# Down weights stored in the steps' order, early additions without priority, and a rearranged last normalization, in a two-layer decoder trunk

## The chip, the core and the metric

The kernel runs on one core of a Trainium2 chip. The metric is the device time of one execution, in microseconds. The engines are PE (TensorE, matmuls; PEld is its weight load), DVE (VectorE), ACT (ScalarE), POOL (GpSimd) and SP (SyncE, which here issues nearly all DMAs). Each engine works through its own instructions in order and waits on semaphores for the others. PSUM, into which TensorE writes, has eight banks.

## The reference

The reference is a decoder trunk of two layers on a sequence of 1024 positions with 1024 channels. Each layer adds a mixer and then a dense MLP to the residual h, each behind an RMS norm, and a last RMS norm gives the output:

```python
for layer in range(DEPTH):
    y = _rms_norm(h, mix_norm_g[layer])
    ...                      # gated spatial mixer, then dilated attention
    h = h + y
    y = _rms_norm(h, mlp_norm_g[layer])
    h = h + jnp.square(jax.nn.relu(y @ w_up[layer])) @ w_down[layer]
return _rms_norm(h, final_norm_g)
```

The hidden width is 4096. Everything is float32 and h is held transposed: eight tiles h[0] to h[7] of 128 channels by 1024 positions.

## The kernel before

**Products.** A float32 matmul is made from three matmuls of a reduced type: each operand is split into a high part (a ScalarE copy, line 205) and a low part (source minus high part, on VectorE, line 206), and high·high, high·low and low·high are added in PSUM (`three`). Weights appear in the profile as `wp` when split and as `r` when just loaded; hidden activations as `hx` when split and `t` when loaded.

**The MLP.** Both products of the MLP are done with seven block products in place of eight, each a 2x2 scheme (Strassen-like, with the terms numbered 1 to 7 in the code). For every group of weights, `Weights` loads four blocks into staging buffers (SP, line 169), GpSimd forms four sums and differences (lines 410, 411, 412 and 415), and ScalarE and VectorE split seven blocks in the order 4, 1, 2, 5, 6, 7, 3. The `steps` of the next group are called between the products of the present one, so one group is prepared while the other is multiplied.

**The down projection** (`Down.run`) goes through 18 steps t. Step t works for output rows a = t mod 4, that is the tiles h[a] and h[a + 4], and sums over a window of up to four hidden groups: one group in step 0, two in step 1, three in step 2, four from step 3 on. The groups are taken in the order 14, 0, 1, 2 ... 13, since 14 is still on the chip when the up projection ends; the others are read back from DRAM (`hid`). Within a step the products go in the order of terms 5, 6, 1, 7, 3, 2, 4. Term 5 writes a PSUM bank d, which is then added to one half of h[a + 4] (`add(1, 1, d)`, line 940); term 3 accumulates into the same bank, and d is added to another half (`add(0, 1, d)`). Terms 7 and 4 share a bank e, terms 1 and 2 a bank a. So term 3 waits for the addition that follows term 5, and term 4 for the one that follows term 7. Term 6 goes with an accumulator u that lives across steps (lines 954, 962, 963, 966).

**What sets the order.** TensorE's order is written out by the program as it runs through a simple model of time. The orders of the other engines come from a list scheduler with its own estimates, in which `tc.high_priority` moves an instruction forward. The additions to h on VectorE had this priority in every step; the splits of weights and hidden tiles had none. SP's order comes from the same scheduler.

**The end.** After step 17 the hidden group 15 is multiplied (`close`), first for positions 0 to 511, then for 512 to 767, then for 768 to 1023. After each piece `final` normalizes it: squares of h, sums over channels by matmuls with a vector of ones, `rsqrt` (a root on ScalarE and five small VectorE instructions, lines 236 to 246), a `spread` of the result over a PSUM bank by transposes on TensorE (line 187), and the products, each followed by a store. Some tiles, those in `far`, are multiplied by GpSimd (line 1591): ScalarE has multiplied them by the gain (line 1579), and GpSimd multiplies by `pc`, a copy of the spread that ScalarE makes in SBUF (line 1586). The others go through VectorE (line 1593), which reads the spread in PSUM. In the last piece (`Direct`) the sums run along with the matmuls: each block of 128 positions has a PSUM bank of its own, and VectorE copies the two columns together (line 309).

Of the kernel before, what the change touches and what calls it, by code (L numbers as in the profile page):

```python
# [12 lines left out]
AF = mybir.ActivationFunctionType  # L13
# [4 lines left out]
P = 128  # L18
D = 1024
S = 1024  # L20
HALF = 512
KT = D // P
# [11 lines left out]
def blk(b, n=1):  # L34
    return slice(b * P, (b + n) * P)
# [69 lines left out]
PRIO = 60  # L105
# [7 lines left out]
def trunk(ctx: ExitStack, tc: tile.TileContext, xT, w_u, w_v, w_o, w_s, b_s, w_qkv, w_bo, rel,  # L113
          w_up, w_dn, w_dl, vecs, onehot, outT):
    nc = tc.nc
# [12 lines left out]
    def temp():  # L128
        return tpool.tile([P, HALF], F32, tag="t", name="t", bufs=NT)
# [46 lines left out]
    def at_bank():  # L176
        return psa.tile([P, HALF], F32, tag="at", name="at")

    def matmul(out, lhsT, rhs, passes=1, **kw):
        nc.tensor.matmul(out, lhsT, rhs, **kw)  # L180
        n = 1
        for d in rhs.shape[1:]:
            n *= d
        flow.pe(max(n, 64) * COL * passes)
# [9 lines left out]
    ones = const.tile([P, P], F32, name="ones")  # L194
# [34 lines left out]
    def rsqrt(src, scale, out=None, power=False):  # L229

        n = src.shape[1]
        v = small.tile([P, n], F32, tag="rv", name="rv")
        r = small.tile([P, n], F32, tag="rr", name="rr")
        if not power:
            sd = small.tile([P, n], F32, tag="sd", name="sd")
            nc.scalar.activation(sd, src, AF.Sqrt, bias=eps, scale=scale)
        nc.vector.tensor_scalar(v, src, scale, EPS, op0=ALU.mult, op1=ALU.add)
        if power:
            nc.gpsimd.tensor_tensor(r, v, mhalf[:, 0:n], op=ALU.pow)
        else:  # L240
            nc.vector.reciprocal(r, sd)
        a = small.tile([P, n], F32, tag="ra", name="ra")
        nc.vector.tensor_tensor(a, r, v, op=ALU.mult)
        nc.vector.scalar_tensor_tensor(a, a, -0.5, r, op0=ALU.mult, op1=ALU.mult)
        q = small.tile([P, n], F32, tag="rq", name="rq") if out is None else out
        nc.vector.scalar_tensor_tensor(q, a, 1.5, r, op0=ALU.add, op1=ALU.mult)
        return q
# [37 lines left out]
    class Direct(Square):  # L285


        def __init__(self, cols):
            super().__init__(cols)
            self.parts, self.ps = [], [at_bank() for _ in range(self.n // P)]  # L290

        def add(self, k):
            sq = temp()[:, 0:self.n]
# [3 lines left out]
                self.sum(k - 2)  # L297

        def sum(self, k):
            for b, ps in enumerate(self.ps):  # L300
                matmul(ps[:, 0:1], self.parts[k][:, blk(b)], ones[:, 0:1], passes=2, start=k == 0, stop=k == KT - 1)

        def rms(self, out=None):
            for k in range(KT - 2, KT):
                self.sum(k)
            with tc.high_priority(offset=PRIO):
                v = temp()[:, 0:len(self.ps)]
                for b, ps in enumerate(self.ps):
                    nc.vector.tensor_copy(v[:, b:b + 1], ps[:, 0:1])
                return rsqrt(v, 1.0 / D, out)  # L310

    def spread(r):

# [570 lines left out]
    class Down:  # L884
# [12 lines left out]
        def weights(self, t, **kw):  # L897
            a, ks = self.todo[t]

            runs = []  # L900
            for k in (self.order[i] for i in ks):
                if runs and k == runs[-1][1]:
                    runs[-1][1] += 1
                else:
                    runs.append([k, k + 1])
            return Weights(lambda i, j: [w_dn[self.layer, a, i, j][:, lo * P:hi * P] for lo, hi in runs], **kw)

        def take(self, k, src, which):
            for p in which:
# [16 lines left out]
        def run(self, w):  # L926
            for t, (a, ks) in enumerate(self.todo):
# [8 lines left out]
                    return [self.x[self.order[k]][p] for k in ks]  # L936

                def add(i, s, src, engine=nc.vector):
                    with tc.high_priority(offset=PRIO if engine is nc.vector else 0):
                        engine.tensor_tensor(hs[i, s], hs[i, s], src, op=ALU.add)  # L940

                if t == 16:
# [630 lines left out]
    def final(sq):  # L1573
        n, far = HALF // sq.n, {}

        for k in {0: (1, 3, 5), 512: (0, 4), 768: (0,)}[sq.cols.start]:
            far[k] = temp().rearrange("p (k t) -> p k t", k=n)
            for i in range(n):
                nc.scalar.activation(far[k][:, i, :], h[k + i][:, sq.cols], AF.Copy, scale=vec[:, 4, k + i:k + i + 1])
        r = sq.rms()  # L1580
        yield LAT["rms"]
        pb = spread(r)
        out = outT.rearrange("(k p) t -> p k t", p=P)
        pc = spare()[:, 0:sq.n] if far else None
        if far:
            nc.scalar.activation(pc, pb[:, 0:sq.n], AF.Copy)
        for k in range(0, KT, n):
            t = far[k] if k in far else temp().rearrange("p (k t) -> p k t", k=n)
            for i in range(n):
                if k in far:  # L1590
                    nc.gpsimd.tensor_tensor(t[:, i, :], t[:, i, :], pc, op=ALU.mult)
                else:
                    nc.vector.scalar_tensor_tensor(t[:, i, :], h[k + i][:, sq.cols], vec[:, 4, k + i:k + i + 1],
                                                   pb[:, 0:sq.n], op0=ALU.mult, op1=ALU.mult)
            nc.sync.dma_start(out[:, k:k + n, sq.cols], t)
            yield LAT["out"]
# [73 lines left out]
```

## Time and profile before

| | us |
|---|---|
| median of 3 runs | 2140.34 |
| lowest, highest | 2135.99, 2142.17 |
| profiled execution | 2137.66 |
| its span, first to last instruction | 2135.9 |
| TensorE busy in the span | 2103.7 (98%) |
| VectorE, ScalarE, GpSimd busy | 1602.5, 1117.9, 561.8 |

Layer 0's down projection begins at about 611 us and layer 1's at about 1808 us; the last piece's sums end near 2125.6 us. In a row of a profile `h<-h,at` reads: the instruction writes a tile named h from a tile h and a PSUM tile at; `128x512` is partitions by elements; `x3` a count; a bracket gives the idle time of the engine before the instruction, and what ended it. The names at and mm are PSUM banks.

### The profile page before, as it was taken

How to read it: one execution, taken by the hardware profiler on the slowest of the kernel's cores; microseconds unless marked ns; L12 is line 12 of the kernel's file. 1: busy time of each engine (PE TensorE's matmuls, PEld its weight loads, DVE VectorE, ACT ScalarE, POOL GpSimd, SP SyncE). 2: the span in 40 equal slices, each digit the busy share in tenths (PEclk: the TensorE clock that was granted, in tenths of full speed). 3: DMA queues.
4: the chain of work that ended last, by engine and by line, in shares of the span. 5: the costliest groups of instructions: out<-in, count | busy, mean ns of one | idle time of the engine just before them, and what ended most of it. 6: DMA issues, size and time to landing. Idle time of an engine off the chain costs nothing.

```text
span 2135.9 us, 30439 instructions
## 1 busy us (share of the span) xinstructions
PE 2103.7 (98%) x10426; PEld 1742.5 (82%) x10426; DVE 1602.5 (75%) x2918; ACT 1117.9 (52%) x2262; POOL 561.8 (26%) x417
## 2 busy tenths in 40 slices
PE   8999999999999999999999999999999999999998
PEld 7888887888878888887888788888888887888887
DVE  7975258577689888888676867768876667988886
ACT  6644136554574444356666656665555546544443
POOL 2100213233323322531212122201133332332345
PEclk9999999999999999999999999999999999999999
DMA  6411114455354443311112021141155543544432
GB/s 220 141 64 50 40 42 136 161 183 188 129 183 163 158 159 129 103 79 52 46 46 55 32 57 41 47 146 68 52 175 182 194 153 133 192 162 138 142 107 79
DMA packets 158815, 247.07 MB, mean 116 GB/s; under 512 B 33481, under 2 KB 47940, under 8 KB 158660
## 3 DMA queue, kind: packets, MB, share of 16 engines
q1 hardware_dynamic: 158336, 244.94, 35.2%
q8 instruction: 82, 1.34, 0.3%
q14 instruction: 73, 0.60, 0.1%
q10 hardware_dynamic: 324, 0.18, 0.0%
HBM read 180.41 MB, written 64.66 MB: 115 GB/s over the span
## 4 chain that ended last, share of the span: by engine, by line
PE 89%; DVE 6%; ACT 3%; issue 1%; DMA 1%; SPq 0%; DVEq 0%; ACTq 0%
PE at L180 43%; PE mm L180 43%; PE at L187 2%; DVE wp L206 1%; DMA t<-hid 1%; DVE t L206 1%; ACT t L1272 1%; DVE h L340 0%; ACT wp L205 0%; DVE y L206 0%; DVE h L940 0%; DVE tr L206 0%; DVE raws L498 0%; SPq L169 0%; DVE hx L206 0%
## 5 line engine op out<-in xcount | busy, mean ns | idle before, releaser
L205 ACT ACTIVATE wp<-r 128x512 fp32r<-128x512 f32 (+3 forms) x490 | 294.4, 605 | 460.4 <-PE at L180 286.3
L180 PE MATMUL at<-hx,wp 128*128 128x512 f32 x1770 | 413.7, 389 | 3.9 <-DVE wp L206 2.3
L206 DVE TENSOR_TENSOR wp<-r,wp 128x512 fp32r<-128x512 f32 (+3 forms) x490 | 372.7, 764 | 39.3 <-ACT wp L205 36.1
L180 PE MATMUL mm<-y,wp 128*128 128x512 f32 x1608 | 398.2, 393 | 2.3 <-ACT t L1132 1.1
L180 PEld LDWEIGHTS at<-hx,wp 128*128 128x128 f32 x1770 | 331.8, 188 | 75.1 <-DVE h L940 3.3
L180 PEld LDWEIGHTS mm<-y,wp 128*128 128x128 f32 x1608 | 299.3, 188 | 67.8 <-DVE h L340 1.6
L180 PE MATMUL at<-t,wp 128*128 128x512 f32 x1344 | 314.0, 389 | 0.7 <-DVE t L803 0.7
L180 PEld LDWEIGHTS at<-t,wp 128*128 128x128 f32 x1344 | 252.3, 188 | 53.4 <-DVE t L803 1.1
L410 POOL TENSOR_TENSOR t<-r 128x512 f32<-128x512 f32 (+3 forms) x78 | 113.6, 1456 | 679.9 <-DMA r<-in_w_dn 258.5
L412 POOL TENSOR_TENSOR r<-r 128x512 f32<-128x512 f32 (+3 forms) x77 | 113.0, 1468 | 377.6 <-DVE wp L206 344.8
L180 PE MATMUL mm<-t,wp 128*128 128x512 f32 x768 | 191.5, 396 | 0.0
L206 DVE TENSOR_TENSOR hx<-t,hx 128x512 fp32r<-128x512 f32 x192 | 181.0, 955 | 5.5 <-ACT hx L205 5.4
L180 PE MATMUL mm<-hx,wp 128*128 128x512 f32 x708 | 171.7, 389 | 0.0
L180 PEld LDWEIGHTS mm<-t,wp 128*128 128x128 f32 x768 | 140.5, 188 | 29.7 <-DVE t L1207 0.2
L269 POOL TENSOR_TENSOR t<-t 128x512 f32<-128x512 f32 (+1 forms) x54 | 72.3, 1339 | 346.3 <-ACT t L258 344.4
L180 PE MATMUL mm<-y,whi 128*128 128x512 f32 x512 | 158.3, 390 | 0.0
L180 PEld LDWEIGHTS mm<-hx,wp 128*128 128x128 f32 x708 | 132.8, 188 | 27.9 <-DVE b L966 0.4
L940 DVE TENSOR_TENSOR h<-h,at 128x512 f32<-128x512 f32 x144 | 97.5, 679 | 55.4 <-PE at L180 55.4
L803 DVE TENSOR_TENSOR t<-t,at 128x512 f32<-128x512 f32 x116 | 79.1, 683 | 78.2 <-PE at L180 78.0
L180 PE MATMUL at<-y,wp 128*128 128x512 f32 x552 | 137.5, 390 | 0.0
L205 ACT ACTIVATE hx<-t 128x512 fp32r<-128x512 f32 x192 | 118.8, 629 | 31.1 <-DMA t<-hid 26.9
L415 POOL TENSOR_TENSOR r<-r 128x512 f32<-128x512 f32 (+3 forms) x77 | 105.4, 1368 | 85.5 <-issue 53.0
(224 smaller groups left out, 3148.8 us busy)
## 6 DMA issues: line engine op xcount, KB each, us to landing
t<-hid SPq DMA_DIRECT2D x194, 256.0 KB, 5.0
hid<-t SPq DMA_DIRECT2D x140, 256.0 KB, 2.3
r<-in_w_up SPq DMA_DIRECT2D x128, 256.0 KB, 2.7
r<-in_w_dn SPq DMA_DIRECT2D x88, 256.0 KB, 2.6
r<-in_w_qkv SPq DMA_DIRECT2D x72, 256.0 KB, 2.6
hid<-b SPq DMA_DIRECT2D x56, 256.0 KB, 2.9
r<-in_w_v SPq DMA_DIRECT2D x48, 256.0 KB, 3.6
h<-in_xT SPq DMA_DIRECT2D x16, 256.0 KB, 3.8
```

Of the source, the lines that this page charges most:

```text
L180: nc.tensor.matmul(out, lhsT, rhs, **kw)
L187: nc.tensor.transpose(out, src, ident)
L205: nc.scalar.activation(hi, src, AF.Copy)
L206: nc.vector.tensor_tensor(lo, src, hi.bitcast(F32), op=ALU.subtract)
L269: nc.gpsimd.tensor_tensor(self.acc, self.acc, sq, op=ALU.add)
L410: tt(r7, r[0, 0], r[1, 0], op=ALU.subtract)
L412: tt(r6, r[1, 0], r[0, 0], op=ALU.subtract)
L415: tt(r3, r[0, 1], r6, op=ALU.subtract)
L803: nc.vector.tensor_tensor(out, x, y, op=ALU.add)
L940: engine.tensor_tensor(hs[i, s], hs[i, s], src, op=ALU.add)
L1272: nc.scalar.activation(p[:, c], p[:, c], AF.Exp, bias=m, scale=-1.0, accum_out=dn)
```

## The change

There are four edits. The down weights are rolled by one hidden group on the host, so that group 14 lies in front of group 0; a step's groups are then one piece in DRAM, and `weights` loads each block with one DMA in steps 1 to 3, where it took two. The additions to h on VectorE lose their priority in steps 0 and 1. In the first piece of the last norm GpSimd takes a fourth of the eight tiles, tile 7. In the last piece the sums of both blocks go to two columns of one PSUM bank, from which `rsqrt` reads directly without copies; and `spread` is done a second time for `pc`, into a bank of its own.

```diff
         def __init__(self, cols):
             super().__init__(cols)
-            self.parts, self.ps = [], [at_bank() for _ in range(self.n // P)]
+            self.parts, self.ps, self.nb = [], at_bank(), self.n // P
...
         def sum(self, k):
-            for b, ps in enumerate(self.ps):
-                matmul(ps[:, 0:1], self.parts[k][:, blk(b)], ones[:, 0:1], passes=2, start=k == 0, stop=k == KT - 1)
+            for b in range(self.nb):
+                matmul(self.ps[:, b:b + 1], self.parts[k][:, blk(b)], ones[:, 0:1], passes=2, start=k == b == 0,
+                       stop=k == KT - 1, skip_group_check=True)
...
             with tc.high_priority(offset=PRIO):
-                v = temp()[:, 0:len(self.ps)]
-                for b, ps in enumerate(self.ps):
-                    nc.vector.tensor_copy(v[:, b:b + 1], ps[:, 0:1])
-                return rsqrt(v, 1.0 / D, out)
+                return rsqrt(self.ps[:, 0:self.nb], 1.0 / D, out)
...
             a, ks = self.todo[t]
-            runs = []
-            for k in (self.order[i] for i in ks):
-                if runs and k == runs[-1][1]:
-                    runs[-1][1] += 1
-                else:
-                    runs.append([k, k + 1])
-            return Weights(lambda i, j: [w_dn[self.layer, a, i, j][:, lo * P:hi * P] for lo, hi in runs], **kw)
+            return Weights(lambda i, j: w_dn[self.layer, a, i, j][:, ks[0] * P:(ks[-1] + 1) * P], **kw)
...
                 def add(i, s, src, engine=nc.vector):
-                    with tc.high_priority(offset=PRIO if engine is nc.vector else 0):
+                    with tc.high_priority(offset=PRIO if engine is nc.vector and t > 1 else 0):
                         engine.tensor_tensor(hs[i, s], hs[i, s], src, op=ALU.add)
...
-        for k in {0: (1, 3, 5), 512: (0, 4), 768: (0,)}[sq.cols.start]:
+        for k in {0: (1, 3, 5, 7), 512: (0, 4), 768: (0,)}[sq.cols.start]:
...
         if far:
-            nc.scalar.activation(pc, pb[:, 0:sq.n], AF.Copy)
+            nc.scalar.activation(pc, (spread(r) if sq.cols.stop == S else pb)[:, 0:sq.n], AF.Copy)
...
-        "w_dn": dn[..., 0:15, :].reshape(2, 4, 2, 2, P, 15 * P),
+        "w_dn": np.roll(dn[..., 0:15, :], 1, axis=5).reshape(2, 4, 2, 2, P, 15 * P),
```

TensorE's order stays as it was but for two more transposes at the very end. The orders of the others shift at three places that matter below. The first is VectorE's queue in step 0 of the down projection in layer 0 (h_94 is h[0], h_98 is h[4], the 128x256 rows are the splits of step 1's weights in the order 4, 1, 2, 5, 6, 7, b is u). Before:

```order
L206 TENSOR_TENSOR wp<-r,wp 128x256
L940 TENSOR_TENSOR h_98<-h_98,at 128x512
L206 TENSOR_TENSOR wp<-r_5571,wp 128x256
L963 TENSOR_TENSOR b<-b,at 128x512
L940 TENSOR_TENSOR h_98<-h_98,at 128x512
L940 TENSOR_TENSOR h_94<-h_94,at 128x512
L940 TENSOR_TENSOR h_94<-h_94,mm 128x512
L940 TENSOR_TENSOR h_98<-h_98,at 128x512
L206 TENSOR_TENSOR wp<-r,wp 128x256
L206 TENSOR_TENSOR wp<-r_5571,wp 128x256
L206 TENSOR_TENSOR wp<-r,wp 128x256
L206 TENSOR_TENSOR wp<-t,wp 128x256
```

The same queue after the change:

```order
L206 TENSOR_TENSOR wp<-r,wp 128x256
L932 TENSOR_TENSOR h_98<-h_98,at 128x512
L206 TENSOR_TENSOR wp<-r_5571,wp 128x256
L206 TENSOR_TENSOR wp<-r,wp 128x256
L932 TENSOR_TENSOR h_98<-h_98,at 128x512
L955 TENSOR_TENSOR b<-b,at 128x512
L206 TENSOR_TENSOR wp<-r_5571,wp 128x256
L206 TENSOR_TENSOR wp<-r,wp 128x256
L206 TENSOR_TENSOR wp<-t,wp 128x256
L932 TENSOR_TENSOR h_94<-h_94,at 128x512
L206 TENSOR_TENSOR wp<-r_5571,wp 128x256
L932 TENSOR_TENSOR h_94<-h_94,mm 128x512
```

Splits 2, 5, 6 and 7 stand in front of additions that they stood behind. The second place is VectorE's queue in step 1, where the 128x384 rows are the splits of step 2's weights and h_99 is h[5]; the first h_99 row is the addition after term 5, the second the one after term 7. Before:

```order
L206 TENSOR_TENSOR wp<-r,wp 128x384
L940 TENSOR_TENSOR h_99<-h_99,at 128x512
L206 TENSOR_TENSOR wp<-r_5641,wp 128x384
L206 TENSOR_TENSOR hx<-t,hx 128x512
L206 TENSOR_TENSOR wp<-r,wp 128x384
L206 TENSOR_TENSOR hx<-t,hx 128x512 x2
L963 TENSOR_TENSOR b<-b,at 128x512
L940 TENSOR_TENSOR h_99<-h_99,at 128x512
```

The same queue after the change:

```order
L206 TENSOR_TENSOR wp<-r,wp 128x384
L206 TENSOR_TENSOR wp<-r_5637,wp 128x384
L932 TENSOR_TENSOR h_99<-h_99,at 128x512
L206 TENSOR_TENSOR hx<-t,hx 128x512
L955 TENSOR_TENSOR b<-b,at 128x512
L206 TENSOR_TENSOR wp<-r,wp 128x384
L206 TENSOR_TENSOR hx<-t,hx 128x512
L206 TENSOR_TENSOR wp<-r_5637,wp 128x384
L206 TENSOR_TENSOR hx<-t,hx 128x512
L206 TENSOR_TENSOR wp<-r,wp 128x384
L932 TENSOR_TENSOR h_99<-h_99,at 128x512
```

Two more splits stand in front of the second h_99 row. The third place is VectorE's queue at the end, from the last tile products of the piece 512 to 767 through the rsqrt of the last piece. Before:

```order
L1593 SCALAR_TENSOR_TENSOR t<-h_14113,vec,at 128x256
L1593 SCALAR_TENSOR_TENSOR t<-h_14119,vec,at 128x256
L309 COPY t<-at 128x1 x2
L1593 SCALAR_TENSOR_TENSOR t<-h_14121,vec,at 128x256
L237 TENSOR_SCALAR rv<-t 128x2
L241 RECIPROCAL rr<-sd 128x2
L243 TENSOR_TENSOR ra<-rr,rv 128x2
L244 SCALAR_TENSOR_TENSOR ra<-ra,rr 128x2
L246 SCALAR_TENSOR_TENSOR rq<-ra,rr 128x2
```

The same queue after the change:

```order
L1585 SCALAR_TENSOR_TENSOR t<-h_14099,vec,at 128x256
L1585 SCALAR_TENSOR_TENSOR t<-h_14101,vec,at 128x256
L237 TENSOR_SCALAR rv<-at 128x2
L241 RECIPROCAL rr<-sd 128x2
L1585 SCALAR_TENSOR_TENSOR t<-h_14107,vec,at 128x256
L243 TENSOR_TENSOR ra<-rr,rv 128x2
L1585 SCALAR_TENSOR_TENSOR t<-h_14109,vec,at 128x256
L244 SCALAR_TENSOR_TENSOR ra<-ra,rr 128x2
L246 SCALAR_TENSOR_TENSOR rq<-ra,rr 128x2
```

The two copies are gone, and two tile products stand between the small steps of rsqrt.

## The prediction

> **What bounds the kernel now.** I read the page's summary first, then the busy time by stretches, then the waits of TensorE in the stretches where it is not full, then the timeline there and at the end.
>
> ```profile
> span 2135.9 us, 30439 instructions
> PE 2103.7 (98%) x10426; PEld 1742.5 (82%) x10426; DVE 1602.5 (75%) x2918; ACT 1117.9 (52%) x2262; POOL 561.8 (26%) x417
> ```
>
> TensorE is busy for 2103.7 of 2135.9 us, and the change takes no matmul away (it adds two transposes). So all that can be won is some of the 32 us in which TensorE idles, and only where the change touches it: the start of the down projection in each layer, and the last microseconds. Two rows of the view by stretches hold the first place (columns: stretch, length, then busy us and instruction counts of PE, PEld, DVE, ACT and POOL, the clock, the DMA share, GB/s).
>
> ```profile
> 611.70:640.70 29.00, 27.08 (x118) 21.46 (x116) 28.25 (x44) 20.27 (x40) 13.52 (x12) 1.00 0.69 228
> 1808.20:1837.30 29.10, 27.08 (x118) 21.48 (x116) 28.40 (x44) 20.25 (x40) 13.49 (x12) 1.00 0.68 228
> ```
>
> These are steps 0 to 2 in layer 0 and in layer 1. TensorE loses 29.00 - 27.08 = 1.92 us in the one and 29.10 - 27.08 = 2.02 in the other, 3.94 together, at full clock. VectorE is busy for 28.25 of the 29.00: here VectorE sets the pace. The waits of TensorE around the first of them (sum, number of times, longest):
>
> ```profile
> PE at L180 <- DVE wp L206: 1.1, 1, 1.1
> PE at L180 <- DVE h L940: 0.8, 1, 0.8
> ```
>
> and where they lie on the timeline (start, length, engine, and in brackets the idle time before):
>
> ```profile
> 612.27 0.88 DVE L206 TENSOR_TENSOR wp<-r,wp 128x256 fp32r<-128x256 f32 x1
> ...
> 615.70 0.99 PEld L180 LDWEIGHTS at<-hx,wp 128*128 128x128 f32 x5 [0.42 <-DVE h L940]
> ...
> 617.36 1.15 DVE L206 TENSOR_TENSOR wp<-r,wp 128x256 fp32r<-128x256 f32 x3
> ...
> 618.23 2.58 PE L180 MATMUL at<-hx,wp 128*128 128x512 f32 x10 [1.10 <-DVE wp L206]
> ...
> 621.16 0.68 DVE L206 TENSOR_TENSOR hx<-t,hx 128x512 fp32r<-128x512 f32 x1
> ...
> 624.86 0.67 DVE L940 TENSOR_TENSOR h<-h,at 128x512 f32<-128x512 f32 x1
> ...
> 626.09 5.60 PE L180 MATMUL at<-hx,wp 128*128 128x512 f32 x24
> ...
> 639.94 0.67 DVE L940 TENSOR_TENSOR h<-h,at 128x512 f32<-128x512 f32 x1
> ...
> 640.66 7.78 PE L180 MATMUL at<-hx,wp 128*128 128x512 f32 x33 [0.81 <-DVE h L940]
> ```
>
> At 617.1 step 1's first product waits 1.10 us for the low half of its weights (the second of the three splits at 617.36), which stood on VectorE behind the five additions of step 0. At 639.9 step 2's last product, term 4 in the bank of term 7, waits 0.81 us for the addition that empties that bank (639.94); Between term 7 and term 4 TensorE works through two products of nine matmuls, 18 x 5.60/24 = 4.2 us, so term 7 was done by 635.7 and this is a queue on VectorE and no dependence on fresh data. Layer 1 repeats both.
>
> **The down steps, part by part.** What VectorE does in the first of the two stretches, by shape (count, busy us and mean ns, idle before it):
>
> ```profile
> L206 DVE TENSOR_TENSOR hx<-t,hx 128x512 fp32r<-128x512 f32 x9 | 7.6, 856 | 0.0
> L940 DVE TENSOR_TENSOR h<-h,at 128x512 f32<-128x512 f32 x10 | 6.7, 675 | 0.0
> L206 DVE TENSOR_TENSOR wp<-r,wp 128x384 fp32r<-128x384 f32 x6 | 4.0, 666 | 0.5 <-ACT wp L205 0.5
> L206 DVE TENSOR_TENSOR wp<-r,wp 128x256 fp32r<-128x256 f32 x6 | 2.8, 500 | 0.0
> L206 DVE TENSOR_TENSOR wp<-t,wp 128x256 fp32r<-128x256 f32 x1 | 0.4, 411 | 0.0
> L963 DVE TENSOR_TENSOR b<-b,at 128x512 f32<-128x512 f32 x2 | 1.4, 680 | 0.3 <-ACT b L962 0.3
> ```
>
> First, the wait at 617.1. Between split 1 and split 5 of step 1 stood five additions (u and four to h) and split 2; now two additions and split 2. Three additions of 0.675 go out of the way: split 5 ends 2.0 us earlier, near 616.1. Without the 0.42 us that the weight load waits at 615.70 for an addition, which now follows fewer instructions too, TensorE wants it at about 616.4. So 1.10 + 0.42 = 1.5 us goes here in each layer.
>
> Second, what is late next. The addition of term 7 of step 1 (the second h_99 row) now stands behind five 128x384 splits and not three. That is 2 x 0.51 = 1.0 us more in front of it (0.51 is an estimate for a 384 split that nothing holds up: three quarters of the 0.68 of a 512 split in the row at 621.16 below). Before, it ended at 624.86 + 0.67 = 625.53, and TensorE reached the term that needs it at 626.09, without a wait. Now TensorE arrives at 626.09 - 1.5 = 624.6 and the addition ends at 625.5 + 1.0, less the idle time that VectorE no longer has. That idle time is 29.00 - 28.25 = 0.75 us. If it all goes, the addition ends at 625.8 and term 4 starts just after: of the 1.5 us some 0.3 is left. Queued behind that term are all of step 2's matmuls.
>
> Third, the addition at 639.94. The instructions in front of it on VectorE are the same set as before, in another order. It can come earlier only by VectorE's idle time and by how long its splits are held up. So it moves by at most 0.75 us if nothing is held longer, and TensorE's 0.81 us there shrinks by as much. Is the idle time really gone? It came late from the loads:
>
> ```profile
> SPq L169 <- DVE wp L206: 13.0, 7, 6.5
> 618.73 1.30 ACT L205 ACTIVATE hx<-t 128x512 fp32r<-128x512 f32 x2 [1.50 <-DMA t<-hid]
> 618.16 9.26 SPq L169 DMA_DIRECT2D r<-in_w_dn  x10
> ```
>
> The order of the down weights takes 12 DMAs out of each layer (steps 1 to 3, four blocks each, one piece in place of two). Six of them stood on SP in front of the hidden tiles that ScalarE waits 1.50 us for at 618.73; SP spends 9.26 us on the ten at 618.16, waits and all, and the bare issue of one is 0.89/2 = 0.45 us (the row at 2130.46 below), so those tiles are asked for up to 2.7 us earlier. SP's larger wait, 13.0 us, is for the staging buffers, which VectorE's splits empty; splits that stand earlier empty them earlier. I take 0.7 us of the 0.75 as gone.
>
> Against that stands how long a split is held. The two rows that show it:
>
> ```profile
> 634.35 1.61 POOL L412 TENSOR_TENSOR r<-r 128x512 f32<-128x512 f32 x1 [3.57 <-DVE wp L206]
> 634.73 1.77 DVE L206 TENSOR_TENSOR hx<-t,hx 128x512 fp32r<-128x512 f32 x1
> ```
>
> A split under GpSimd's work takes 1.77 us where an undisturbed one takes 0.68, and ends with a short rest behind GpSimd's end; an addition from PSUM keeps its 0.675 all through the stretch (ten of them in 6.7 us). At 612.27 a 128x256 split takes 0.88 in place of 0.41, also under GpSimd. The change moves splits 2, 5, 6 and 7 forward by up to 2 us, nearer to the time in which GpSimd forms the combinations of step 1 and 2 (612.1 to 617.5), where the additions stood that lose nothing. From below, none of them meets GpSimd: 0. From above, all four are held as the one at 612.27: 4 x 0.47 = 1.9 us. GpSimd's own work starts earlier as well, since its first input lands earlier, so I take nothing beyond the present for the sum and keep 1.9 for the range.
>
> The Trainium skill, page "SBUF — State Buffer", section "Who interferes with whom", says that a VectorE instruction with two SBUF inputs is locked out by a GpSimd instruction that reads SBUF for that one's whole length, and that one with a single SBUF input is not. The rows agree (1.77 against 0.675). By that rule as it stands, the four splits moved into GpSimd's time would cost the 1.9 us above in each layer, and the sum would be a loss of some 2.6 us with the end; it is the second rival.
>
> So each layer gives 0.7 us, between -1.2 (0.7 less 1.9) and 1.97 (all of its waits), and both give **1.4 us**.
>
> **The end.**
>
> ```profile
> 2112.40 1.94 ACT L1579 ACTIVATE t<-h,vec 128x512 f32<-128x512 f32 x3
> ...
> 2114.79 2.37 POOL L269 TENSOR_TENSOR t<-t 128x256 f32<-128x256 f32 x3 [1.39 <-ACT t L258]
> ...
> 2115.07 0.60 PE L187 MATMUL at<-ident,rq 128*128 128x128 f32 x4
> ...
> 2117.73 0.95 PE L180 MATMUL at<-ones,t 128*128 128x1 f32 x8
> ...
> 2123.26 0.38 PE L187 MATMUL at<-ident,rq 128*128 128x128 f32 x2
> ...
> 2124.19 2.79 POOL L1591 TENSOR_TENSOR t<-t,b 128x256 f32<-128x256 f32 x4 [3.31 <-issue]
> ...
> 2125.01 0.61 PE L180 MATMUL at<-ones,t 128*128 128x1 f32 x4 [0.23 <-ACT t L294]
> 2126.20 0.21 DVE L309 COPY t<-at 128x1 f32<-128x1 f32 x2
> 2126.45 0.29 ACT L236 ACTIVATE sd<-t,scalars 128x2 f32<-128x2 f32 x1 [0.69 <-DVE t L309]
> 2127.50 0.16 DVE L246 SCALAR_TENSOR_TENSOR rq<-ra,rr 128x2 f32<-128x2 f32 x1
> 2127.81 0.66 PE L187 MATMUL at<-ident,rq 128*128 128x128 f32 x2 [2.19 <-DVE rq L246]
> 2128.56 0.38 ACT L1586 ACTIVATE b<-at 128x256 f32<-128x256 f32 x1 [1.81 <-PE at L187]
> 2129.02 1.41 POOL L1591 TENSOR_TENSOR t<-t,b 128x256 f32<-128x256 f32 x2 [2.04 <-ACT b L1586]
> 2130.46 0.89 SPq L1595 DMA_DIRECT2D outT<-t  x2
> ```
>
> The fourth GpSimd tile costs VectorE one product less and GpSimd one more. GpSimd idles 3.31 us before 2124.19, which hides it. Its scaling on ScalarE is a fourth instruction of 1.94/3 = 0.65 us, ahead of the squares that GpSimd's sums at 2114.79 wait for. These end at 2117.16 and TensorE wants them at 2117.73: 0.57 us of cover, so 0.1 us shows.
>
> The shared bank takes the two copies out. The root starts when the sums end, 2125.62, and not at 2126.45; but the order now puts two tile products of about 0.4 between the small steps of rsqrt, and the first small step follows the root, since both read one bank. 2125.66 + 0.29 + two steps of 0.15 + 2 x 0.4 + three of 0.16 + some 0.2 of issue is 2127.45, where rq now ends at 2127.66: 0.2 us won.
>
> The second spread lets VectorE go without ScalarE's copy (0.4 us earlier), but of the last four stores on SP's queue GpSimd's comes first: 2130.46 is just behind GpSimd's end at 2129.02 + 1.41. GpSimd waits for the copy, and the copy now for two more transposes. They cost (0.60 - 0.38)/2 = 0.11 each at full clock and about twice that where two take 0.66: between 0.22 and 0.44, taken as 0.3. The end gives 0.1 - 0.2 + 0.3 = **0.2 us lost**, between 0.6 won (the root starts 2126.45 - 2125.62 = 0.83 earlier, the tile products cost nothing, the transposes 0.22) and 0.6 lost (0.1, 0.44 for the transposes, and a chain no shorter than now).
>
> **Sum.** The profiled execution took 2137.66 us, span and launch; 2137.66 - 1.4 + 0.2 = 2136.5. It lies 2.7 below the median of the runs, 2140.34 (2135.99 to 2142.17), and the forecast for a median is **2139.1 us**.
>
> **The rivals.**
>
> All waits go, chance 0.17: the splits meet GpSimd less than now and the addition of term 7 is never late. Then 3.94 us and at the end 0.6 go: 2140.34 - 4.5 = 2135.8. Against it speaks that VectorE has 0.75 us of slack in 29.
>
> The late additions and held splits cost more than the early splits bring, chance 0.18: place, step 1's term 4 and step 2's term 4, both behind VectorE. It decides from the point at which the splits are held for more than 0.75 us longer in a layer. At 1.9 each layer loses 1.2, and with 0.6 at the end that is 2140.34 + 3.0 = 2143.3. For it speaks the 1.77 row; against it, that GpSimd starts earlier.
>
> The change does nothing there, chance 0.2: the staging buffers (the 13.0 us) hold the loads as before, the wait at 617.1 turns up whole at step 1's term 4, and the end is even: 2140.3.
>
> **Chances and range.** The forecast has 0.45. A measurement of this kernel cannot tell less than 0.3% (6.4 us) from none. No case reaches that: the most that can be won is 4.5 us, and for a loss of 6.4 each layer would have to lose 3. So within 0.3% 0.90, faster 0.05 and slower 0.05, for mechanisms that I don't see and for the scatter of the medians. The range takes in both outer cases and about 2 us of scatter at the lower end: 2133.5 to 2144.
>
> **What would show it.** TensorE's wait for L206's wp at step 1 is gone, and one of about 1.2 us for an addition to h appears 8 us later. The wait at step 2's term 4 shrinks to a few tenths or stays below 1 us. VectorE stays above 95% busy in the stretch; 128x256 splits with a mean over 0.6 us would be the second rival. The copies at L309 are gone, rq ends some 1.8 us after the last sums, and the last four stores still begin at GpSimd's end. A difference of more than 5 us, or TensorE losing time anywhere else, would make the account wrong.

## The result: 0.3% slower, outside the range

The changed kernel takes 2146.8 us (median of 12 runs, 2142.05 to 2148.78), the kernel before in the same comparison 2140.03 (12 runs). The ratio is 1.0029, with a 95% interval of 1.0021 to 1.0037. That is about 6.2 us more, and the interval lies wholly above 1. The forecast was 2139.1 and the range ended at 2144.

The profiled execution took 2147.87 us. Its summary:

```profile
span 2146.1 us, 30394 instructions
PE 2108.4 (98%) x10428; PEld 1746.5 (81%) x10428; DVE 1604.3 (75%) x2915; ACT 1118.4 (52%) x2263; POOL 564.6 (26%) x418
```

TensorE does the same work and is *busy* for 4.7 us longer (2108.4 against 2103.7), so it ran more slowly somewhere. The waits of TensorE around the first steps of the down projection in layer 0 (in all, times, longest):

```profile
PE at L180 <- DVE h L932: 3.1, 2, 2.8
```

and in layer 1:

```profile
PE at L180 <- DVE h L932: 3.4, 1, 3.4
```

The wait for `wp` at step 1 is gone, as forecast, and the one at step 2's term 4 as well. One wait for an addition to h took their place, of 2.8 and 3.4 us and not of 1.2. This is the place on the timeline of layer 0 (step 0 began 0.75 us earlier than in the run before):

```profile
611.52 1.00 DVE L206 TENSOR_TENSOR wp<-r,wp 128x256 fp32r<-128x256 f32 x1
...
613.04 1.57 DVE L206 TENSOR_TENSOR wp<-r,wp 128x256 fp32r<-128x256 f32 x2
...
615.27 3.82 PE L180 MATMUL at<-hx,wp 128*128 128x512 f32 x15 [0.28 <-DVE h L932]
615.73 1.62 DVE L206 TENSOR_TENSOR wp<-r,wp 128x256 fp32r<-128x256 f32 x2
...
624.61 1.74 POOL L408 TENSOR_TENSOR t<-r 128x512 f32<-128x512 f32 x1 [1.55 <-DMA r<-in_w_dn]
...
625.15 1.62 DVE L206 TENSOR_TENSOR wp<-r,wp 128x384 fp32r<-128x384 f32 x1
...
626.69 0.68 DVE L932 TENSOR_TENSOR h<-h,at 128x512 f32<-128x512 f32 x1
...
627.42 7.37 PE L180 MATMUL at<-hx,wp 128*128 128x512 f32 x24 [2.83 <-DVE h L932]
```

Two things stand there. The last 128x384 split in front of the addition after term 7 (626.69) takes 1.62 us in place of 0.55, since GpSimd's first sum for step 3 runs from 624.61. In the run before that sum came behind the addition (which ended at 625.53) and fell on another split:

```profile
627.92 1.29 POOL L410 TENSOR_TENSOR t<-r 128x512 f32<-128x512 f32 x1 [5.20 <-DMA r<-in_w_dn]
628.19 1.43 DVE L206 TENSOR_TENSOR wp<-t,wp 128x384 fp32r<-128x384 f32 x1
```

And the 24 matmuls behind the wait take 7.37 us, where the prediction quotes 5.60 for the same 24. The view by stretches shows why. Its rows are three stretches of 3.41 us: the one with the gap, and the two after it (the last columns are the granted clock, the DMA share, GB/s):

```profile
624.20:627.61 3.41, 0.57 (x3) 0.19 (x2) 3.41 (x5) 0.52 (x1) 2.92 (x2) 1.00 0.26 77
627.62:631.03 3.41, 3.41 (x9) 2.66 (x9) 3.41 (x6) 0.80 (x2) 0.27 (x1) 0.50 0.84 259
631.04:634.45 3.41, 3.41 (x17) 2.77 (x16) 2.43 (x5) 1.61 (x3) 0.00 (x0) 1.00 0.98 353
```

For 3.41 us after the gap TensorE has a clock of 0.50 and starts 9 matmuls, then 17 in as long. Below, such a stretch is called a half clock.

In layer 1 two splits in a row are held in front of that addition, each beside a sum of GpSimd:

```profile
1826.78 1.47 POOL L408 TENSOR_TENSOR t<-r 128x512 f32<-128x512 f32 x1 [1.16 <-DMA r<-in_w_dn]
1827.04 1.76 DVE L206 TENSOR_TENSOR hx<-t,hx 128x512 fp32r<-128x512 f32 x1
...
1828.33 1.59 POOL L409 TENSOR_TENSOR r<-r,r 128x512 f32<-128x512 f32 x1
1828.72 1.61 DVE L206 TENSOR_TENSOR wp<-r,wp 128x384 fp32r<-128x384 f32 x1
```

The end, for comparison with the rows of the prediction:

```profile
2134.36 0.61 PE L180 MATMUL at<-ones,t 128*128 128x1 f32 x4 [0.38 <-ACT t L294]
2135.00 0.26 ACT L236 ACTIVATE sd<-at,scalars 128x2 f32<-128x2 f32 x1 [0.69 <-PE at L180]
...
2136.96 0.16 DVE L246 SCALAR_TENSOR_TENSOR rq<-ra,rr 128x2 f32<-128x2 f32 x1
2137.27 1.09 PE L187 MATMUL at<-ident,rq 128*128 128x128 f32 x4 [2.30 <-DVE rq L246]
...
2138.91 1.41 POOL L1583 TENSOR_TENSOR t<-t,b 128x256 f32<-128x256 f32 x2 [2.47 <-ACT b L1578]
```

**Where the span's 10.2 us come from.** I compared the start of the same matmul, counted from the program's start, in both traces. The down projection's first five steps lose 2.7 us in layer 0 and 2.4 in layer 1, and from the last sums to GpSimd's end the last piece takes 5.96 us in place of 5.42, 0.5 more. Those are 5.7 us at places that the change touches, near the 6.2 of the medians. The rest stands elsewhere: 1.6 us in small pieces between 700 and 1545, and 2.75 in layer 1's up projection, where a wait of 1.81 us (0.7 before) was followed by a half clock too. What is left of the 10.2, a gain of 0.75 ahead of step 0 and losses near the end, nearly cancels. Other kernels below have or lack such losses elsewhere, as their runs fell.

### The profile page after: what moved, and what is told of

The parts are those of the page before. It is cut to its first block, busy times and chain, and to the rows that moved or that the text cites. A ratio compares the mean times of both kernels' runs of the same rounds, so it can differ in the third digit from the quotient of the medians.

```text
span 2146.1 us, 30394 instructions
## 1 busy us (share of the span) xinstructions
PE 2108.4 (98%) x10428; PEld 1746.5 (81%) x10428; DVE 1604.3 (75%) x2915; ACT 1118.4 (52%) x2263; POOL 564.6 (26%) x418
## 4 chain that ended last, share of the span: by engine, by line
PE 89%; DVE 6%; ACT 3%; DMA 1%; issue 1%; SPq 0%; DVEq 0%; ACTq 0%
PE at L180 44%; PE mm L180 43%; PE at L187 2%; DVE wp L206 1%; DVE t L206 1%; DVE h L338 1%; ACT t L1264 0%; ACT wp L205 0%; DVE y L206 0%; DVE tr L206 0%; DVE h L932 0%; DMA h<-hd 0%; DMA t<-hid 0%; DVE raws L496 0%; DMA t<-bvec 0%
```

## The experiments

In the list below "stage" is how much later (+) or earlier (-) the matmul after step 4 starts, with the start of step 0 as zero, against the trace of before: layer 0, layer 1. "Clock loss" is (1 - mean granted clock) x mean span over all timed runs of the kernel; since each run gives its clock to three decimals, take it as good to a few tenths. In the profiled runs 3.6 to 5.8 us of it belong to the half clock that sets in near the last sums, where TensorE has almost nothing left to do, so only its differences tell something.

| kernel | median us | ratio (95%) | stage us | clock loss us | rest of span us |
|---|---|---|---|---|---|
| before | 2139.7 to 2140.0 | 1 | 0, 0 | 7.3 to 7.8 | 2130.3 to 2131.1 |
| the change | 2146.80 | 1.0029 (1.0021 to 1.0037) | +2.7, +2.4 | 12.3 | 2132.2 |
| e1 edit 2 alone | 2143.59 | 1.0021 (1.0012 to 1.0029) | +2.7, +1.9 | 9.7 | 2132.5 |
| e2 edit 1 alone | 2136.86 | 0.9984 (0.9975 to 0.9993) | -0.6, -1.6 | 6.0 | 2128.9 |
| e3 the end alone | 2141.27 | 1.0003 (0.9994 to 1.0012) | +0.6, +0.4 | 8.0 | 2131.1 |
| e4 two exceptions | 2139.96 | 0.9999 (0.9990 to 1.0008) | +2.3, -1.0 | 8.0 | 2130.1 |
| e5 filler matmuls | 2146.28 | 1.0026 (1.0016 to 1.0036) | +2.8, +2.6 | 9.6 | 2135.0 |
| e6 GpSimd held back | 2139.36 | 0.9997 (0.9988 to 1.0006) | 0.0, -0.9 | 8.4 | 2129.9 |
| e7 priority lost in step 0 only | 2139.25 | 0.9991 (0.9982 to 0.9999) | -0.2, -1.0 | 7.8 | 2129.0 |
| e8 e4 without the end | 2139.18 | 0.9993 (0.9983 to 1.0002) | +0.3, -0.1 | 7.8 | 2129.4 |
| e9 e8, step 4 reordered | 2136.52 | 0.9982 (0.9973 to 0.9991) | -0.8, -2.4 | 7.2 | 2127.7 |
| e10 step 0's last three | 2136.34 | 0.9987 (0.9978 to 0.9996) | -1.2, -2.1 | 8.3 | 2127.3 |

Of the 6.4 us that the mean span of the change lies above the 2138.1 of before, 4.5 are clock loss (12.3 - 7.8) and 1.9 the rest. The stages come from one profiled run of each kernel. In e3 VectorE's order in these steps is that of before, and its stages still differ by 0.6 and 0.4 us: so much is scatter.

**e1, e2, e3: the parts alone.** e1 is before with the priority rule of edit 2, e2 with the new order of the down weights and its loads, e3 with the three edits at the end.

```diff
# e1, on before
-  with tc.high_priority(offset=PRIO if engine is nc.vector else 0):
+  with tc.high_priority(offset=PRIO if engine is nc.vector and t > 1 else 0):
# e2, on before
-  return Weights(lambda i, j: [w_dn[self.layer, a, i, j][:, lo * P:hi * P] for lo, hi in runs], **kw)
+  return Weights(lambda i, j: w_dn[self.layer, a, i, j][:, ks[0] * P:(ks[-1] + 1) * P], **kw)
-  "w_dn": dn[..., 0:15, :].reshape(2, 4, 2, 2, P, 15 * P),
+  "w_dn": np.roll(dn[..., 0:15, :], 1, axis=5).reshape(2, 4, 2, 2, P, 15 * P),
# e3, on before
-  self.parts, self.ps = [], [at_bank() for _ in range(self.n // P)]
+  self.parts, self.ps, self.nb = [], at_bank(), self.n // P
...
-  for k in {0: (1, 3, 5), 512: (0, 4), 768: (0,)}[sq.cols.start]:
+  for k in {0: (1, 3, 5, 7), 512: (0, 4), 768: (0,)}[sq.cols.start]:
-  nc.scalar.activation(pc, pb[:, 0:sq.n], AF.Copy)
+  nc.scalar.activation(pc, (spread(r) if sq.cols.stop == S else pb)[:, 0:sq.n], AF.Copy)
```

> The kernel before with one edit alone: the additions to h lose their priority in steps 0 and 1; weights are loaded in two pieces as before, the end is as before. Theory A (the late addition): TensorE waits some 2 to 3 us for the addition after term 7 of step 1 in both layers, the clock record shows a half-speed piece of 3.41 us behind each of the two waits, and the time is about 5 us above before (2145). Theory B (the early loads: GpSimd's first sum for step 3 comes earlier and holds the last split in front of that addition): the loads stay late here, so the wait is shorter by the 1.07 us of that held split, under 1.8 us, no half-speed piece follows, and the time is within 2 us of before.

> The kernel before with one edit alone: the down weights rolled by one group, one DMA per block in steps 1 to 3; every addition keeps its priority. Theory A: neither wait grows, VectorE idles less, the time is 0 to 2 us under before. Theory B: GpSimd's earlier sums hold VectorE's splits here too; a wait of over 1.5 us appears in step 1 or 2 and the time is 1 to 3 us above before.

> The kernel before with the three edits of the end alone (fourth GpSimd tile, one bank for the sums, second spread); the down steps as before. Theory A and B alike: no change outside the last 35 us. From the profile of the change the end is 0.5 to 0.8 us longer, which cannot be told in the time (within 0.1% of before, 2140 to 2141.5); if the end were the cause of the loss, 4 us or more.

Edit 1 alone wins (0.9984), edit 2 alone loses (1.0021), the end can't be told from nothing. In e1 the loss already comes one product group earlier, at step 0's term 4. Its timeline in layer 0:

```profile
614.87 2.52 DVE L206 TENSOR_TENSOR wp<-r,wp 128x256 fp32r<-128x256 f32 x3
615.18 0.79 POOL L415 TENSOR_TENSOR r<-r 128x256 f32<-128x256 f32 x1
615.94 1.17 POOL L410 TENSOR_TENSOR t<-r 128x384 f32<-128x384 f32 x1
...
617.31 0.68 DVE L940 TENSOR_TENSOR h<-h,at 128x512 f32<-128x512 f32 x1
...
618.04 5.30 PE L180 MATMUL at<-hx,wp 128*128 128x512 f32 x15 [2.43 <-DVE h L940]
```

Three splits that take 0.41 each when nothing holds them stand in front of an addition without priority and last 2.52 us beside GpSimd; TensorE waits 2.43 for the addition, and its clock is 0.50 for the next 3.41 us here too. (Layer 1 has the same wait of 2.43 us at the same place, but no half clock.) Both theories of e1 looked for the late addition in step 1; it stands in step 0. So the change's loss doesn't come from edit 1 and edit 2 meeting alone: edit 2 loses in any case, and together they lose at another addition. e2 still waits 1.3 and 1.2 us for `wp` at step 1, but its two stages together are 2.2 us shorter.

**e4: the change, with priority kept for two additions.** In steps 0 and 1 the additions after terms 5 and 7 (`i == s == 1`) keep it; the second of these is what TensorE waits for in the change.

```diff
-  with tc.high_priority(offset=PRIO if engine is nc.vector and t > 1 else 0):
+  with tc.high_priority(offset=PRIO if engine is nc.vector and (t > 1 or i == s == 1) else 0):
```

> The changed kernel, but the additions after terms 5 and 7 keep their priority in steps 0 and 1, since terms 3 and 4 wait for them in the same banks; only the other three additions of a step go without. Theory A: the wait at 617 stays away as in the change, the wait of 2.8 us goes too, no half-speed piece is left in the down steps, and the time is 2 to 4 us under before and 8 to 10 under the change. Theory B: the splits are held as in the change, a wait of at least 1 us stays in step 1, and the time is not under before.

The waits of 2.8 and 3.4 us go and 0.5 and 0.9 for `wp` remain, no half clock follows, and 6.8 us of the change's time go with them (2139.96); the 2 to 4 us under before that theory A expected do not come. Up to 650 us layer 0 is even 1.4 us ahead of before. But at 675.9, in step 4, a new wait takes it back:

```profile
675.90 4.62 PE L180 MATMUL mm<-hx,wp 128*128 128x512 f32 x12 [1.86 <-DVE b L958]
```

Twelve matmuls in 4.62 us and not 2.88: this gap halved the clock as well.

**e5: no gap for TensorE.** The changed kernel, with matmuls whose result nobody reads in place of the gap.

```diff
+                if t == 1:
+                    spin = mm_bank()
+                    for _ in range(12):
+                        matmul(spin, w[4].hi[:, blk(0)], xs(4)[0].hi, start=True, stop=True)
                 product(e, w[4], xs(4), True)
```

> The changed kernel with twelve more 128x512 matmuls ahead of term 4 of step 1, in each layer, into a bank that nobody reads (12 x 0.23 = 2.8 us, as long as TensorE waits there under the change). They add no wait of their own as long as the bank is free, and TensorE has no gap. Theory A (part of the loss is the clock: the gap of 2.83 and 3.4 us halves it for 3.41 us, which costs 1.7 us a layer): no stretch at half clock in either down projection, the 24 matmuls behind the addition take about 5.6 us and not 7.4, and the time falls by 2 x 1.7 = 3.4 us from the change's 2146.8 to about 2143.4, 1.0016 of before. Theory B (the half clock there has nothing to do with the gap, or costs nothing): the stretch stays, or goes and leaves the time at 2146.8 or above, 1.0031 or more.

Its timeline in layer 0:

```profile
622.92 4.24 PE L180 MATMUL mm<-hx,wp 128*128 128x512 f32 x18
...
624.63 1.86 POOL L408 TENSOR_TENSOR t<-r 128x512 f32<-128x512 f32 x1 [1.60 <-DMA r<-in_w_dn]
...
625.25 1.65 DVE L206 TENSOR_TENSOR wp<-r,wp 128x384 fp32r<-128x384 f32 x1
...
626.83 0.67 DVE L932 TENSOR_TENSOR h<-h,at 128x512 f32<-128x512 f32 x1
...
627.56 5.73 PE L180 MATMUL at<-hx,wp 128*128 128x512 f32 x24 [0.40 <-DVE h L932]
```

This tells the two costs apart. The split is held as before (1.65), the addition comes at the same time (626.83), and term 4 starts within 0.14 us of where it started in the change. But the 24 matmuls now take 5.73 and not 7.37: the half clock is worth 1.64 us, and it comes from the gap. Over the timed runs the clock loss falls from 12.3 to 9.6. That part is theory A. The time, however, is theory B's: 2146.28. In the profiled run what was won is lost again in step 4, where TensorE waits 1.48 us (layer 0) and 0.8 (layer 1) for the accumulator b, and 1.2 us of the wait at step 1 are left in layer 1. The rest of the span is 2.8 us up. Behind step 1 the scheduler also put a few of VectorE's instructions in another order, so whether b would be late without that stays open; e8 and e9 take it up.

**e6: GpSimd's sum behind the addition.** The changed kernel, with one GpSimd copy of a single column that must wait for the addition after term 7.

```diff
                 add(1, 1, e)
+                if t == 1:
+                    with tc.high_priority(offset=PRIO):
+                        nc.gpsimd.tensor_copy(temp()[:, 0:1], hs[1, 1][:, 0:1])
```

> The changed kernel with one more GpSimd copy of one column, which reads the tile of h after the late addition (term 7 of step 1), so that GpSimd's first 128x512 sum for step 3 can begin only behind that addition; in the change it ran from 624.61 beside the split directly ahead of the addition, which took 1.62 us in place of 0.55. Theory A (GpSimd holds the split): the split takes 0.55, the addition comes 1.07 us earlier, TensorE waits about 1.8 us in layer 0 and 2.3 in layer 1 in place of 2.83 and 3.4. If these still halve the clock the time falls by 2.1 us to 2144.7 (1.0021 of before), if they don't by 2 x (1.07 + 1.7) = 5.5 to 2141.3 (1.0006). Theory B (the split is slow for another reason, or the queue of splits alone is the cost): the wait stays at 2.8 and 3.4 and the time at 2146.8.

Timeline in layer 0:

```profile
625.38 0.55 DVE L206 TENSOR_TENSOR wp<-r,wp 128x384 fp32r<-128x384 f32 x1
625.84 0.68 DVE L932 TENSOR_TENSOR h<-h,at 128x512 f32<-128x512 f32 x1
...
626.57 5.74 PE L180 MATMUL at<-hx,wp 128*128 128x512 f32 x24 [1.80 <-DVE h L932]
626.58 0.45 POOL L968 COPY t<-h 128x1 f32<-128x1 f32 x1 [3.22 <-DVE h L932]
```

As theory A said, the split takes 0.55 and the wait is 1.80 us. It is 1.2 in layer 1, where 2.3 was expected: there the change holds two splits, for 1.76 and 1.61 us in place of 0.68 and 0.55, and 3.35 - 2.14 is 1.2. No half clock follows in either layer. The median is 7.4 us under the change, 2 us more than the better branch of theory A; with one instruction of 0.45 us in each layer the whole loss is gone. (On VectorE the order up to the addition is that of the change; from step 2 on it differs a little, so the 2 us may lie there.) Theory B, that the queue of splits alone is the cost, falls.

**e7: priority lost in step 0 alone.**

```diff
-  with tc.high_priority(offset=PRIO if engine is nc.vector and t > 1 else 0):
+  with tc.high_priority(offset=PRIO if engine is nc.vector and t > 0 else 0):
```

> The changed kernel in which additions to h lose their priority in step 0 alone; step 1 keeps it. Theory A (what costs is the addition after term 7 of step 1, which waits behind splits): TensorE's wait of 2.8 and 3.4 us goes, no half clock there, about 2 x 2.7 + 2 x 1.0 = 7 us under the change, near 2139.5, 0.9997 of before. Theory B (what costs is the loss of priority in step 0, whose additions then crowd step 1): at least half of the loss stays, 2144 or above, 1.0018 or more.

2139.25, theory A within 0.3 us: the cost is the addition of step 1. Now step 1 waits for a split again, 1.3 us in layer 1 and in layer 0:

```profile
PE at L180 <- DVE wp L206: 1.4, 1, 1.4
PE at L180 <- DVE h L932: 0.3, 1, 0.3
```

**e8, e9, e10: is there a version that keeps both gains?** e8 is edit 1 with e4's two exceptions and the old end; e9 adds to it a one-column copy on GpSimd in step 4; e10 is edit 1 with priority taken only from step 0's last three additions.

```diff
# e9, on e8: behind step 4's first addition to b
+                        if t == 4:
+                            nc.gpsimd.tensor_copy(temp()[:, 0:1], self.u[a][:, 0:1])
# e10, on e2
-  with tc.high_priority(offset=PRIO if engine is nc.vector else 0):
+  with tc.high_priority(offset=PRIO if engine is nc.vector and (t > 0 or i == s == 1) else 0):
```

> Edit 1 (down weights in the steps' order) with early additions losing priority except the two to the tile that step 1's term 4 waits for (after terms 5 and 7); the end is left as before. Theory A (edit 1 wins, edit 2 wins where it doesn't delay that addition; the end costs about 0.7): a little under edit 1 alone (2136.9), by what the stages showed, 1.0 in layer 0 and 0.2 in layer 1: 2135.7, 0.998 of before. Theory B (the two edits collide on VectorE wherever the priority goes, as with the wait of 1.86 us at 675.9 in step 4 of layer 0 when the end was changed too): 2138 to 2140, 0.999 to 1.000.

> The kernel of edit 1 with the two exceptions (e8_keep_layout), and one more GpSimd copy of one column in step 4, which reads the sum b after VectorE's first addition to it, so that GpSimd's four sums of that step begin behind that addition; without it they began at 665.79 and held two splits ahead of it for 3.48 us, and TensorE waited 1.61 and 1.7 us for b. Theory A (the down projection's gain is given back there, because GpSimd holds those splits): the wait for b goes, each layer keeps what it won before step 4, and the time falls by about 1.6 + 1.7 = 3.3 us to 2135.9, 0.998 of before. Theory B (VectorE has no room there: the sums then hold other splits, or come too late for their own readers): another wait of about 1.6 us stands in step 4 or 5 and the time stays near 2139.2, 0.9995.

> Edit 1, with priority taken only from the three last additions to h of step 0 (after terms 3, 2 and 4; the two to the tile of step 1's term 4 keep it); step 1 and the end as before. Theory A (edit 2's gain lies in step 0 alone, its cost in step 1): the wait of 1.3 and 1.2 us for a split that edit 1 alone leaves at step 1's term 4 shrinks to under 0.5, and nothing is late behind it: 2136.9 - 1.7 = 2135.2, 0.998 of before. Theory B (what is won there is given back in step 4, as with the two exceptions, by a wait of about 1.6 us for b): 2138 to 2139, 0.9993.

e8 fits theory B: the waits at step 1 are down to 0.3 and 0.2, and step 4 takes back 1.6 and 1.7 us. Its timeline there:

```profile
668.88 1.63 POOL L412 TENSOR_TENSOR r<-r 128x512 f32<-128x512 f32 x1
669.27 3.48 DVE L206 TENSOR_TENSOR hx<-t,hx 128x512 fp32r<-128x512 f32 x2
...
672.67 0.68 DVE L948 TENSOR_TENSOR b<-b,at 128x512 f32<-128x512 f32 x1
...
675.08 0.68 DVE L960 TENSOR_TENSOR b<-b,mm 128x512 f32<-128x512 f32 x1
...
675.81 3.01 PE L180 MATMUL mm<-hx,wp 128*128 128x512 f32 x12 [1.61 <-DVE b L960]
```

e9 did what theory A wanted, in another way than I had meant. The copy landed behind the four sums and not ahead of them, so GpSimd's sums are where they were; but it made the scheduler put splits behind the additions to b. One held split and not two stands in front of the first addition, and one split and not three between the first and the second:

```profile
669.18 1.79 DVE L206 TENSOR_TENSOR hx<-t,hx 128x512 fp32r<-128x512 f32 x1
...
670.89 0.67 DVE L948 TENSOR_TENSOR b<-b,at 128x512 f32<-128x512 f32 x1
671.49 1.18 DVE L206 TENSOR_TENSOR wp<-r,wp 128x512 fp32r<-128x512 f32 x1
672.75 0.69 DVE L962 TENSOR_TENSOR b<-b,mm 128x512 f32<-128x512 f32 x1
...
674.11 2.88 PE L180 MATMUL mm<-hx,wp 128*128 128x512 f32 x12
```

b is ready at 673.44 and not 675.76 (0.75 us of that is an earlier start of the whole stage), TensorE doesn't wait, and the time falls by 2.7 us to 2136.52. That the splits ahead of b gave the gain back is thus shown. How much of it was GpSimd holding them, and how much their number, is not: GpSimd's sums were not moved away from them. e10 reaches 2136.34 with neither the step 4 wait nor more than 0.8 us of waits in the stage of either layer. e2, e9 and e10 beat the kernel before by 0.13 to 0.18%, and their intervals don't tell them from each other.

## Why the prediction was wrong, step by step

**The wait at 617.1** went as said: the 1.10 us for `wp` are gone, though 0.28 us for h remain. TensorE reaches the product ahead of step 1's term 4 earlier by 0.9 us, counted from the start of step 0, where 1.5 was forecast; in layer 1 it is 1.5.

**"What is late next"** is the step that failed. It named the right place, the addition after term 7 of step 1, and the right cause, five splits of 128x384 in front of it. The size was wrong: 1.2 us against 2.83 and 3.35. The term that was missing is the time for which GpSimd holds splits, which the sum took at nothing beyond the present. Measured, the last of the five splits took 1.62 and not 0.55. That is 1.07 of the 1.63 us by which the wait in layer 0 is too long, and e6, which takes it away, leaves a wait of 1.80; where the other 0.6 come from stays open. In layer 1 two splits are held, for 2.14 us more than e6 shows for free ones. That is all of the 2.15 by which its wait is too long, and e6 leaves the forecast's 1.2.

Splits were held further ahead too. In the groups of VectorE's work in this stretch the six of 128x256 went from a mean of 500 to 794 ns:

```profile
L206 DVE TENSOR_TENSOR wp<-r,wp 128x256 fp32r<-128x256 f32 x6 | 4.6, 794 | 0.0
```

That is 6 x 0.294 = 1.8 us more, close to the upper bound of 1.9 that the prediction had worked out for four held splits and then left out of the sum. Little of it seems to have reached the addition: in e6, with the same order on VectorE up to there, the six have a mean of 531 ns, and the addition after term 5 of step 1 begins only 0.35 us earlier (9.62 us after step 0's first matmul, 9.97 in the change).

I took GpSimd's earlier start as a reason for no extra cost. It was the reason for it: the load that lands earlier (edit 1) lets GpSimd's next sum start 2.6 us earlier in the stage (2.9 in e2, which has edit 1 alone), onto a split that stands in front of an urgent addition.

The Trainium skill, page "SBUF — State Buffer", section "Who interferes with whom", states that a VectorE instruction with two SBUF inputs contends with a GpSimd instruction that reads SBUF, and that one with at most one SBUF input, outside some faster modes, does not. The rows above agree: 1.62 beside a sum and 0.55 without one, and the additions from PSUM stay at 0.68.

**The clock** was no step of the prediction at all. It read the waits of before "at full clock" and took that over. A gap of 2.83 us costs 1.64 us more than itself (e5). By that, the two gaps are worth about 3.3 of the 4.5 us of clock loss in the mean spans (2 x 1.64, an estimate). In the profiled run the rest is the half clock at 1562 (1.7 us) and a longer one at the end (0.8). The prediction said that a loss of 0.3% would need 3 us in each layer, and no term of its sum reached that; with the clock it came to 2.7 and 2.4.

**Step 2's term 4** lost its wait, as forecast. That took back 1.1 us of what step 1's term 4 had lost, and is in the stage's +2.7.

**The rivals.** The second one had the mechanism and the place, with its mark of "128x256 splits with a mean over 0.6" (0.794 measured) and its price of 1.2 us a layer; it lacked the clock's 1.6, so its 2143.3 was too low. Its held splits and the end were to cost 3.0 us, and the rest of the span, without the clock, did rise by 1.9. The mark alone doesn't tell the loss: e6, which loses nothing, has 0.643 in layer 1.

**The end.** Forecast 0.2 us lost; measured 0.5 from the last sums on, and 0.4 in the product group ahead of them, which stand in every trace with these edits and in none without; together they pass the 0.6 of its worst case. The group ahead had no term in the sum: VectorE's last addition to h there follows a tile product without a break, where it waited 0.29 us for TensorE before. The root does start when the sums end, but rq ends 2.15 us behind them, not 1.8; before it was 2.04. The prediction's terms for this, added up again, give 2127.73 and not 2127.45, so by them rq was 0.07 us late and not 0.2 early; measured, 0.11 late. The tile products still stand between the small steps and take what the copies had cost. The second spread costs 0.43 us (1.09 against 0.66 for the transposes, both at a clock of 0.50), at the top of its range. As e3 this edit alone is 1.0003, within its interval of nothing.

**No time elsewhere**, the last of the marks, failed in the profiled run: 2.75 us at 1562 and 1.6 before it. The last section shows why the first of these comes and goes.

## What to carry to other kernels

Before taking priority from an instruction, price its queue with every neighbour that can be held, at the held price, above all when the same change makes the other engine's work start earlier. In this kernel a gap of TensorE cost its length, and about 1.7 us more (half of 3.41) where it left TensorE 1.6 us of work or less in one window of the clock. By that, two short waits in different windows should cost less than one long one; no run compares them. When a local gain is shown by one wait going away, follow TensorE on to the next place where the late engine must deliver, here step 4's accumulator, before counting it.

## What the hardware showed unasked

The half clock comes in stretches of 3.413 us, or two of them in a row (6.827 us near 990 in e2, e5 and e10), and within one run all stretches begin on one grid: in the change at 627.62, 1562.88 and 1832.53, which are 274 and 79 lengths apart. In the products of the MLP, where all matmuls are 128x512, what decides is how long TensorE is busy within one such window. Two more windows of the change ahead of a half clock, by the view of stretches:

```profile
1559.47:1562.88 3.41, 1.60 (x8) 1.00 (x7) 3.41 (x5) 0.63 (x1) 2.24 (x2) 1.00 0.72 206
1829.12:1832.53 3.41, 1.54 (x7) 1.28 (x8) 3.41 (x6) 0.00 (x0) 0.80 (x1) 1.00 0.32 87
```

The window of this kind with the least work that no half clock followed, in e8:

```profile
1871.85:1875.26 3.41, 1.66 (x8) 1.07 (x7) 3.41 (x7) 0.63 (x1) 0.00 (x0) 1.00 0.25 73
```

and the one in e6 that holds most of its gap of 1.80 us:

```profile
622.36:625.77 3.41, 2.41 (x11) 1.68 (x9) 3.41 (x7) 1.19 (x3) 1.01 (x1) 1.00 0.20 65
```

Windows with 0.57, 0.98 (e1), 1.52 (e10), 1.54, 1.55 (e4) and 1.60 us of TensorE's work were followed by a half clock, those with 1.66, 1.70 (e1, layer 1), 1.71 (e4), 1.79 (e9), 2.18 (e2) and 2.41 were not; the line lies between 1.60 and 1.66, just under half of 3.41. So the same wait of 1.8 us is free of it in e2 and e6, where the grid cuts the gap in two, and costs about 1.7 us more in the change at 1562 (half of 3.41, an estimate).

Busy time is not the whole rule. Between the two MLPs, where many matmuls are smaller (64x128 and the like), windows with more work were followed by a half clock too, of 1.82 us near 1212 in e7 and 1.91 in e9, and this one in e3:

```profile
993.46:996.87 3.41, 2.65 (x18) 1.58 (x20) 1.58 (x9) 2.60 (x11) 0.00 (x0) 1.00 0.00 0
```

Others there, with 2.04 us (e9 at 1208), were not. What counts in such windows stays open. The grid lies differently in each profiled run, so such waits may add to the scatter of the times; no run here measures how much.

The Trainium skill, page "TensorE: Matmul & The Clock Gate", gives the window in section "What's actually happening" as free-running, with 3413 ns; the grid and the 3.413 us agree. The Trainium skill, page "TensorE: Matmul & The Clock Gate", section "HAM oscillation — how this bites in real kernels", warns of gaps over about 3.4 us; here a gap of 1.81 us was enough.
